# Rotary embedding on one core: the two tables loaded as sixteen rows each and spread by TensorE

## The chip, the cores and the metric

The kernel runs on one core of one Trainium2 chip. The time is what the device needs for one execution, in microseconds (us), as the median of several runs. A profiled execution of the same program gives what each engine and each transfer did; its times are read from the start of the span, that is, from the first to the last instruction.

Five engines work side by side, each through its own list of instructions: TensorE (PE), VectorE (DVE), ScalarE (ACT), GpSimd (POOL) and SyncE (SP). Transfers between memory and SBUF run on sixteen DMA engines, fed here by two queues: one that SyncE issues to (q1, "hardware_dynamic") and one that GpSimd issues to (q0, "software_dynamic"). A transfer that changes the type on its way, such as float32 in memory to float16 in SBUF, is issued by GpSimd here.

## The reference

The rotary embedding of x (8 batches, 2048 positions, 16 heads, 64 elements a head, float32) with tables cos and sin of 2048 x 32 float32:

```
x1 = x[..., :32]
x2 = x[..., 32:]
out1 = x1 * cos - x2 * sin      # cos, sin by position, the same for each batch and head
out2 = x1 * sin + x2 * cos
out = concatenate([out1, out2], axis=-1)
```

x is 67.1 MB and so is the output; a table is 256 KB.

## The kernel before, in words

Each batch is a tile of 128 partitions. Partition p holds the positions 16p to 16p + 15 (J = 16), so 16 x 1024 elements; in memory that is 64 KB in one piece for each partition. The load (`load`, line 54, GpSimd) casts to float16 on the way in, the store (`store`, line 62, GpSimd) casts back to float32 on the way out. The tiles come from a ring of five buffers, `io_pool`, tag "xt".

`rotate` (lines 67 to 83) is three VectorE passes over a tile: line 75 multiplies the swapped halves by the sine with its sign (`sin_h`, 128 x 16 x 64 float16) into `v`, line 81 multiplies the tile by the cosine (`cos_h`, 128 x 512 float16) in place, line 83 adds `v`.

At the start SyncE issues three transfers, in this order: the sine table (line 42, `sin_f`), the first four positions of each partition of batch 0 as float32 (line 43, `head`, 2 MB), and the cosine table (line 47, `cos_f`). A table is loaded as 128 rows of 2 KB, one for each partition: partition p gets its own 16 positions x 32 values. GpSimd at once issues the load of the rest of batch 0 and that of batch 1 (line 54).

ScalarE then makes the float16 tables and casts the head: the sine (line 94), the sine with its sign turned (line 95), position 0 of the head (`narrow_head`, line 89), the cosine (line 97), positions 1 to 3 of the head (line 89 again). VectorE rotates position 0 of batch 0 by itself (`rotate(tiles[0], 0, JF)`, line 99), and GpSimd stores it (line 108) before it issues loads 2, 3 and 4. That order of GpSimd's transfers (load 0, load 1, the first store, loads 2 to 4) is fixed by dependencies that hold no wait ("order of the ring", lines 115 to 121).

After that, batch by batch, VectorE rotates and GpSimd stores; the load of batch b + 5 takes over the buffer of batch b when its store has landed. The last batch goes out in three parts: two by GpSimd (lines 136 and 138), and the last two positions cast to float32 by ScalarE (line 147) and stored by SyncE (line 148), behind the first part.

Of the kernel before, what the change touches and what calls it, by code (L numbers as in the profile page):

```python
# [1 line left out]

# [4 lines left out]


@with_exitstack  # L10
def kernel(
    ctx: ExitStack,
    tc: tile.TileContext,
    x: bass.AP,
    cos: bass.AP,
    sin: bass.AP,
    out: bass.AP,
):
    nc = tc.nc
    f16 = mybir.dt.float16  # L20
    f32 = mybir.dt.float32

    B, S, H, D = x.shape
    Dh = D // 2
    P = nc.NUM_PARTITIONS
    J = S // P
    NBUF = 5

    const_pool = ctx.enter_context(tc.tile_pool(name="rope_const", bufs=1))
    io_pool = ctx.enter_context(tc.tile_pool(name="rope_io", bufs=NBUF))  # L30
    tmp_pool = ctx.enter_context(tc.tile_pool(name="rope_tmp", bufs=1))

    JA = 4
    JE = 2
    JF = 1
    head = io_pool.tile([P, JA, H, D], f32, tag="xt")
    x0 = x[0].rearrange("(p j) h d -> p j (h d)", j=J)
    sin_f = const_pool.tile([P, J, Dh], f32)
    cos_f = const_pool.tile([P, J, Dh], f32)
    cos_h = const_pool.tile([P, J, Dh], f16)  # L40
    sin_h = const_pool.tile([P, J, D], f16)
    nc.sync.dma_start(out=sin_f, in_=sin.rearrange("(p j) d -> p j d", j=J))  # L42
    nc.sync.dma_start(  # L43
        out=head.rearrange("p j h d -> p (j h d)"),
        in_=x0[:, 0:JA, :].rearrange("p j f -> p (j f)"),
    )
    nc.sync.dma_start(out=cos_f, in_=cos.rearrange("(p j) d -> p j d", j=J))

    loads = []

    def load(b):
        xt = io_pool.tile([P, J, H, D], f16, tag="xt")
        j0 = JA if b == 0 else 0
        dma = nc.gpsimd.dma_start(  # L54
            out=xt[:, j0:J, :, :].rearrange("p j h d -> p (j h d)"),
            in_=x[b].rearrange("(p j) h d -> p j (h d)", j=J)[:, j0:J, :].rearrange("p j f -> p (j f)"),
        )
        loads.append(dma)
        return xt

    def store(b, xt, j0=0):
        return nc.gpsimd.dma_start(  # L62
            out=out[b].rearrange("(p j) h d -> p j (h d)", j=J)[:, j0:J, :].rearrange("p j f -> p (j f)"),
            in_=xt[:, j0:J, :, :].rearrange("p j h d -> p (j h d)"),
        )

    def rotate(xt, j0, j1):
        v = tmp_pool.tile([P, J, H, D], f16)
        n = j1 - j0
        js = slice(j0, j1)  # L70
        shape = [P, n, H, 2, Dh]
        sin_b = sin_h[:, js, :].rearrange("p j (e d) -> p j e d", e=2).unsqueeze(2).to_broadcast(shape)
        cos_b = cos_h[:, js, :].unsqueeze(2).to_broadcast([P, n, 2 * H, Dh])
        xe = xt[:, js, :, :].rearrange("p j h (e d) -> p j h e d", e=2)
        nc.vector.tensor_mul(  # L75
            out=v[:, js, :, :].rearrange("p j h (e d) -> p j h e d", e=2),
            in0=xe[:, :, :, ::-1, :],
            in1=sin_b,
        )
        xw = xt[:, js, :, :].rearrange("p j h (e d) -> p j (h e) d", d=Dh)  # L80
        nc.vector.tensor_mul(out=xw, in0=xw, in1=cos_b)  # L81
        xa = xt[:, js, :, :].rearrange("p j h d -> p (j h d)")
        nc.vector.tensor_add(out=xa, in0=xa, in1=v[:, js, :, :].rearrange("p j h d -> p (j h d)"))  # L83


    tiles = [load(0)]
    tiles.append(load(1))
    def narrow_head(j0, j1):
        nc.scalar.copy(  # L89
            out=tiles[0][:, j0:j1, :, :].rearrange("p j h d -> p (j h d)"),  # L90
            in_=head[:, j0:j1, :, :].rearrange("p j h d -> p (j h d)"),
        )

    nc.scalar.copy(out=sin_h[:, :, Dh:D], in_=sin_f)  # L94
    nc.scalar.mul(out=sin_h[:, :, 0:Dh], in_=sin_f, mul=-1.0)  # L95
    narrow_head(0, JF)
    nc.scalar.copy(out=cos_h, in_=cos_f)  # L97
    narrow_head(JF, JA)
    rotate(tiles[0], 0, JF)
    def part(b, j0, j1):  # L100
        return (
            out[b].rearrange("(p j) h d -> p j (h d)", j=J)[:, j0:j1, :].rearrange("p j f -> p (j f)"),
            tiles[b][:, j0:j1, :, :].rearrange("p j h d -> p (j h d)"),
        )

    def store_rows(b, j0, j1):
        dst, src = part(b, j0, j1)
        return nc.gpsimd.dma_start(out=dst, in_=src)  # L108

    first = store_rows(0, 0, JF)  # L110
    ring = [loads[0], loads[1], first]
    for b in range(2, NBUF):
        tiles.append(load(b))
        ring.append(loads[b])
    for a, b in zip(ring[1:], ring[:-1]):
        tc.add_manual_dep(
            a.ins,
            b.ins.name,
            mybir.DependencyInfo(mybir.DependencyClass.NoSync, mybir.DependencyReason.DATA),
            reason="order of the ring",  # L120
        )
    for b in range(B):
        rotate(tiles[b], JF if b == 0 else 0, J)
        if b < B - 1:
            st = store(b, tiles[b], JF if b == 0 else 0)
            if b == 0:
                tc.add_manual_dep(
                    st.ins,
                    first.ins.name,
                    mybir.DependencyInfo(mybir.DependencyClass.NoSync, mybir.DependencyReason.DATA),  # L130
                    reason="order of the ring",
                )
        if b + NBUF < B:
            tiles.append(load(b + NBUF))
    dst, src = part(B - 1, 0, 9)
    gate = nc.gpsimd.dma_start(out=dst, in_=src)  # L136
    dst, src = part(B - 1, 9, J - JE)
    rest = nc.gpsimd.dma_start(out=dst, in_=src)  # L138
    tc.add_manual_dep(
        rest.ins,  # L140
        gate.ins.name,
        mybir.DependencyInfo(mybir.DependencyClass.NoSync, mybir.DependencyReason.DATA),
        reason="order of the ring",
    )
    dst, src = part(B - 1, J - JE, J)
    tail = io_pool.tile([P, JE, H, D], f32, tag="xt")
    nc.scalar.copy(out=tail.rearrange("p j h d -> p (j h d)"), in_=src)  # L147
    end = nc.sync.dma_start(out=dst, in_=tail.rearrange("p j h d -> p (j h d)"))
    tc.add_manual_dep(
        end.ins,  # L150
        gate.ins.name,
        mybir.DependencyInfo(mybir.DependencyClass.Sync, mybir.DependencyReason.DATA),
        reason="the last rows go out behind this part",
    )


# [1 line left out]
_INS = ['x', 'cos', 'sin']  # L158
_OUTS = [((8, 2048, 16, 64), 'float32')]


# [23 lines left out]
```

## Time and profile before

| What | Value |
|---|---|
| Time, median of 3 runs | 316.73 us (316.65 to 316.8) |
| Span of the profiled execution | 314.8 us |
| Time of the profiled execution beside its span | not given on the page; the median of the runs is 1.9 us above the span |
| VectorE busy | 209.1 us (66%), 27 instructions |
| ScalarE busy | 8.6 us (3%), 7 instructions |
| GpSimd busy | 9.9 us (3%), 22 instructions |
| TensorE | no instructions |
| Bytes in memory | 67.63 MB read, 67.11 MB written |
| Sine table: issue to landing | 2.8 us |
| Head: issue to landing | 16.4 us |
| Cosine table: issue to landing | 34.1 us |
| Load 0 (6 MB in memory): issue to landing | 22.0 us |
| First store (512 KB): issue to landing | 6.4 us |
| A VectorE pass over a whole tile, 128 x 16384 | 8.69 us |

The page gives each engine's busy time, the span in 40 slices (a digit is the busy share in tenths), the DMA queues with packets, megabytes and the time their packets took as a share of sixteen engines' span, and the chain of work that ended last. Answers of the trace add a timeline (start, duration, engine and line, what is written from what, and in brackets how long the engine had been idle and what ended that), and sums by stretch (busy time of each engine with the number of instructions in brackets, the clock that TensorE was granted, the DMA engines' share and the GB/s moved). In these GB/s, and in the queues' megabytes, a load that casts to float16 counts with the bytes it writes into SBUF, half of what it reads. Shares of a short stretch can exceed 1, because packets of two queues overlap on an engine.

### The profile page before, as it was taken

The numbers are of one execution on the slowest core, as the hardware profiler recorded it, in microseconds if no ns is written. First come the engines' busy times: TensorE is split into PE (matmuls) and PEld (weight loads), VectorE is DVE, ScalarE is ACT, GpSimd is POOL, SyncE is SP. The second block draws the span as 40 slices with busy tenths as digits, with TensorE's granted clock in tenths as the row PEclk, the third lists the DMA queues.
The fourth block names the chain that finished last, engine by engine and source line by source line (L and its number), as shares of the span: only waits on it lengthen the run. The fifth ranks groups of instructions, "written<-read, shape, count | busy, mean of one in ns | idle before, by whom it ended". The sixth has DMA issues, their size and how long they took to land.

```text
span 314.8 us, 126 instructions
## 1 busy us (share of the span) xinstructions
DVE 209.1 (66%) x27; ACT 8.6 (3%) x7; POOL 9.9 (3%) x22
## 2 busy tenths in 40 slices
DVE  0000299999999999999999999999009993000000
ACT  3010400000000000000000000000000002000000
POOL 1000110000000000010000000200000001000000
DMA  8999999999999899999999999999999999999998
GB/s 262 287 233 212 204 267 200 200 266 200 200 200 325 375 500 400 400 333 266 200 200 208 391 400 400 458 475 266 200 266 466 400 400 516 416 400 400 433 425 341
DMA packets 3168, 102.24 MB, mean 325 GB/s; under 512 B 352, under 2 KB 352, under 8 KB 736
## 3 DMA queue, kind: packets, MB, share of 16 engines
q0 software_dynamic: 2592, 98.57, 97.4%
q1 hardware_dynamic: 576, 3.67, 3.0%
HBM read 67.63 MB, written 67.11 MB: 428 GB/s over the span
## 4 chain that ended last, share of the span: by engine, by line
DMA 39%; DVE 24%; issue 18%; ACT 2%; POOL 0%; SPq 0%; POOLq 0%; DVEq 0%
DMA out_dram<-xt 16%; DMA xt<-in_x_dram 12%; DMA cos_f<-in_cos_dram 11%; DVE xt L83 8%; DVE xt L81 8%; DVE v L75 8%; ACT xt L89 1%; ACT tail L147 1%; POOL out_dram L62 0%; ACT cos_h L97 0%; POOL xt L54 0%; SPq L43 0%; SPq L42 0%; POOLq L54 0%; DVEq L75 0%
## 5 line engine op out<-in xcount | busy, mean ns | idle before, releaser
L75 DVE TENSOR_TENSOR v<-xt,sin_h 128x16384 f16<-128x16384 f16 (+2 forms) x9 | 69.7, 7744 | 35.9 <-ACT xt L89 19.8
L81 DVE TENSOR_TENSOR xt<-xt,cos_h 128x16384 f16<-128x16384 f16 (+2 forms) x9 | 69.7, 7744 | 17.4 <-ACT cos_h L97 17.1
L83 DVE TENSOR_TENSOR xt<-xt,v 128x16384 f16<-128x16384 f16 (+2 forms) x9 | 69.7, 7744 | 0.3
L147 ACT CAST tail<-xt 128x2048 f32<-128x2048 f16 x1 | 1.9, 1898 | 223.7 <-DVE xt L83 223.7
L54 POOL DMA_DIRECT2D xt<-in_x_dram x8 | 4.4, 555 | 105.4 <-DMA out_dram<-xt 104.6
L62 POOL DMA_DIRECT2D out_dram<-xt x7 | 3.7, 535 | 71.4 <-DVE xt L83 71.4
L89 ACT CAST xt<-head 128x1024 f16<-128x1024 f32 (+1 forms) x2 | 3.8, 1896 | 12.9 <-DMA head<-in_x_dram 12.9
L136 POOL DMA_DIRECT2D out_dram<-xt x1 | 0.5, 531 | 41.5 <-DVE xt L83 41.5
L108 POOL DMA_DIRECT2D out_dram<-xt x1 | 0.5, 536 | 35.7 <-DVE xt L83 35.7
L94 ACT ACT_TABLE_LOAD x1 | 1.3, 1283 | 0.7 <-PEq L169 0.7
L97 ACT CAST cos_h<-cos_f 128x512 f16<-128x512 f32 x1 | 0.6, 617 | 17.2 <-DMA cos_f<-in_cos_dram 17.2
L94 ACT CAST sin_h<-sin_f 128x512 f16<-128x512 f32 x1 | 0.6, 617 | 1.5 <-DMA sin_f<-in_sin_dram 1.5
L95 ACT ACTIVATE sin_h<-sin_f 128x512 f16<-128x512 f32 x1 | 0.6, 624 | 0.0
L138 POOL DMA_DIRECT2D out_dram<-xt x1 | 0.5, 531 | 0.0
L169 POOL MEMSET const-float32-0.0<- 128x1 f32 x1 | 0.1, 98 | 0.2 <-issue 0.2
L169 POOL MEMSET const-bfloat16-1.0<- 128x1 bf16 x1 | 0.1, 102 | 0.0
L169 POOL MEMSET const-float32-1.0<- 128x1 f32 x1 | 0.1, 98 | 0.0
L169 POOL MEMSET const-uint8-127<- 128x1 uint8 x1 | 0.1, 98 | 0.0
## 6 DMA issues: line engine op xcount, KB each, us to landing
xt<-in_x_dram POOLq DMA_DIRECT2D x7, 4096.0 KB, 38.3
out_dram<-xt POOLq DMA_DIRECT2D x1, 7680.0 KB, 56.7
out_dram<-xt POOLq DMA_DIRECT2D x1, 4608.0 KB, 42.4
xt<-in_x_dram POOLq DMA_DIRECT2D x1, 3072.0 KB, 22.0
out_dram<-xt POOLq DMA_DIRECT2D x1, 2560.0 KB, 47.9
head<-in_x_dram SPq DMA_DIRECT2D x1, 2048.0 KB, 16.4
out_dram<-tail SPq DMA_DIRECT2D x1, 1024.0 KB, 8.4
out_dram<-xt POOLq DMA_DIRECT2D x1, 512.0 KB, 6.4
```

Source lines behind the costliest of these rows:

```text
L54: dma = nc.gpsimd.dma_start(out=xt[:, j0:J, :, :].rearrange("p j h d -> p (j h d)"), in_=x[b].rearrange("(p j) h d -> p j (h d)", j=J)[:, ...
L62: return nc.gpsimd.dma_start(out=out[b].rearrange("(p j) h d -> p j (h d)", j=J)[:, j0:J, :].rearrange("p j f -> p (j f)"), in_=xt[:, j0:J ...
L75: nc.vector.tensor_mul(out=v[:, js, :, :].rearrange("p j h (e d) -> p j h e d", e=2), in0=xe[:, :, :, ::-1, :], in1=sin_b,)
L81: nc.vector.tensor_mul(out=xw, in0=xw, in1=cos_b)
L83: nc.vector.tensor_add(out=xa, in0=xa, in1=v[:, js, :, :].rearrange("p j h d -> p (j h d)"))
L89: nc.scalar.copy(out=tiles[0][:, j0:j1, :, :].rearrange("p j h d -> p (j h d)"), in_=head[:, j0:j1, :, :].rearrange("p j h d -> p (j h d)"),)
L94: nc.scalar.copy(out=sin_h[:, :, Dh:D], in_=sin_f)
L95: nc.scalar.mul(out=sin_h[:, :, 0:Dh], in_=sin_f, mul=-1.0)
L97: nc.scalar.copy(out=cos_h, in_=cos_f)
L108: return nc.gpsimd.dma_start(out=dst, in_=src)
L136: gate = nc.gpsimd.dma_start(out=dst, in_=src)
L147: nc.scalar.copy(out=tail.rearrange("p j h d -> p (j h d)"), in_=src)
```

## The change

Each table is loaded as sixteen rows of 16 KB instead of 128 rows of 2 KB. Row k holds the positions of partitions 8k to 8k + 7, and lands on partition k of a new tile `wide`, 16 x 2 x 8 x 512 float32, which takes a buffer of the ring (`io_pool`, tag "xt"). VectorE casts a table's part of `wide` to float16 in `narrow`, which shares its buffer with `v`. TensorE then makes the tile of 128 partitions: for each g of 8 one matmul with 512 columns, whose weights `pick[:, g, :]` are 1 where the output partition is 8k + g and 0 elsewhere, all eight summed into one PSUM tile. ScalarE's casts read PSUM instead of `sin_f` and `cos_f`.

`pick` is made from `ones` (set by VectorE) by one select on GpSimd. In the built program GpSimd has two instructions ahead of its first load that it had not before: a reload of its code library and the select. On VectorE the memset of `ones` and the two table casts stand ahead of the first rotation. On ScalarE the second cast of the head now stands ahead of the cast of the cosine; it was behind it. SyncE's order is as before: sine, head, cosine, and at the end the last rows. GpSimd's order of loads and stores is as before.

```
+    K = 16
+    G = P // K
     head = io_pool.tile([P, JA, H, D], f32, tag="xt")
+    wide = io_pool.tile([K, 2, G, J * Dh], f32, tag="xt")
+    narrow = tmp_pool.tile([K, 2, G, J * Dh], f16, tag="v")
-    sin_f = const_pool.tile([P, J, Dh], f32)
-    cos_f = const_pool.tile([P, J, Dh], f32)
+    ones = const_pool.tile([K, G, P], f16)
+    pick = const_pool.tile([K, G, P], f16)
+    psum_pool = ctx.enter_context(tc.tile_pool(name="rope_psum", bufs=1, space=bass.MemoryType.PSUM))
-    nc.sync.dma_start(out=sin_f, in_=sin.rearrange("(p j) d -> p j d", j=J))
+    nc.sync.dma_start(
+        out=wide[:, 0, :, :].rearrange("k g f -> k (g f)"), in_=sin.rearrange("(k r) d -> k (r d)", k=K)
+    )
     nc.sync.dma_start(
         out=head.rearrange("p j h d -> p (j h d)"),
...
-    nc.sync.dma_start(out=cos_f, in_=cos.rearrange("(p j) d -> p j d", j=J))
+    nc.sync.dma_start(
+        out=wide[:, 1, :, :].rearrange("k g f -> k (g f)"), in_=cos.rearrange("(k r) d -> k (r d)", k=K)
+    )
...
-        v = tmp_pool.tile([P, J, H, D], f16)
+        v = tmp_pool.tile([P, J, H, D], f16, tag="v")
...
-    nc.scalar.copy(out=sin_h[:, :, Dh:D], in_=sin_f)
-    nc.scalar.mul(out=sin_h[:, :, 0:Dh], in_=sin_f, mul=-1.0)
+    nc.vector.memset(ones, 1.0)
+    nc.gpsimd.affine_select(
+        out=pick,
+        in_=ones,
+        pattern=[[-1, G], [1, P]],
+        compare_op=mybir.AluOpType.is_equal,
+        fill=0.0,
+        base=0,
+        channel_multiplier=-G,
+    )
+
+    def spread(t):
+        nc.vector.tensor_copy(
+            out=narrow[:, t, :, :].rearrange("k g f -> k (g f)"), in_=wide[:, t, :, :].rearrange("k g f -> k (g f)")
+        )
+        ps = psum_pool.tile([P, J * Dh], f32, tag=f"ps{t}")
+        for g in range(G):
+            nc.tensor.matmul(ps, lhsT=pick[:, g, :], rhs=narrow[:, t, g, :], start=g == 0, stop=g == G - 1)
+        return ps.rearrange("p (j d) -> p j d", j=J)
+
+    sin_p = spread(0)
+    nc.scalar.copy(out=sin_h[:, :, Dh:D], in_=sin_p)
+    nc.scalar.mul(out=sin_h[:, :, 0:Dh], in_=sin_p, mul=-1.0)
     narrow_head(0, JF)
-    nc.scalar.copy(out=cos_h, in_=cos_f)
+    cos_p = spread(1)
+    nc.scalar.copy(out=cos_h, in_=cos_p)
     narrow_head(JF, JA)
```

## The prediction

> **What bounds the kernel now.** I read the page first, then the transfers in two short windows, then the engines and transfers stage by stage, and last the order of the start. The page's transfer lines come first:
>
> ```profile
> DMA  8999999999999899999999999999999999999998
> ...
> q0 software_dynamic: 2592, 98.57, 97.4%
> q1 hardware_dynamic: 576, 3.67, 3.0%
> HBM read 67.63 MB, written 67.11 MB: 428 GB/s over the span
> ```
>
> The sixteen DMA engines are busy in every slice, and the two queues' packets together take the whole span; VectorE has 66%. So the time is bytes over a rate, plus whatever time the DMA engines stand idle. By stages (stretch, length, busy time of DVE, ACT and POOL, clock, DMA share, GB/s on the SBUF side, where a cast load counts half):
>
> ```profile
> 1.75:5.25 3.50, 0.00 (x0) 1.42 (x3) 0.70 (x2) 1.00 1.00 375
> 17.50:42.50 25.00, 5.47 (x4) 4.32 (x3) 2.12 (x4) 1.00 0.97 210
> 42.50:140.00 97.50, 97.12 (x12) 0.00 (x0) 1.61 (x3) 1.00 1.03 307
> 140.00:305.00 165.00, 106.50 (x13) 1.90 (x1) 4.76 (x9) 1.00 1.00 357
> 305.00:313.50 8.50, 0.00 (x0) 0.00 (x0) 0.00 (x0) 1.00 0.98 405
> ```
>
> No stage has a hole. The rate while the engines run is (67.63 + 67.11) MB over 313.5 - 1.8 = 311.7 us, 432 GB/s. The stretch that the change is about, 17.5 to 42.5, looks bad from the compute side and is not:
>
> ```profile
> 3.52 0.62 ACT L94 CAST sin_h<-sin_f 128x512 f16<-128x512 f32 x1 [1.49 <-DMA sin_f<-in_sin_dram]
> ...
> 17.54 1.04 ACT L89 CAST xt<-head 128x1024 f16<-128x1024 f32 x1 [12.87 <-DMA head<-in_x_dram]
> ...
> 35.80 0.62 ACT L97 CAST cos_h<-cos_f 128x512 f16<-128x512 f32 x1 [17.22 <-DMA cos_f<-in_cos_dram]
> ...
> 38.16 0.54 POOL L108 DMA_DIRECT2D out_dram<-xt  x1 [35.71 <-DVE xt L83]
> 38.69 1.59 POOL L54 DMA_DIRECT2D xt<-in_x_dram  x3
> ```
>
> The head lands at 17.5 and the cosine at 35.8, so the first store and the three loads behind it are issued only at 38.16. But GpSimd's queue still holds the second load then: all that is ahead (0.26 + 2.10 + 6.29 + 0.26 + 8.39 = 17.3 MB) takes 40 us at 432 GB/s, to 41.8, and the share over 17.5 to 42.5 is 0.97. The cosine is late by a lot, and nothing in the transfers waits for it.
>
> The start is where something can be lost. Queues with packets in 0 to 5.25, then issues:
>
> ```profile
> q1 hardware_dynamic: 208, 1.31, 66.6%
> ```
>
> ```profile
> 0.74 0.37 SPq L42 DMA_DIRECT2D sin_f<-in_sin_dram  x1
> 1.16 0.42 SPq L43 DMA_DIRECT2D head<-in_x_dram  x1
> 1.25 1.20 POOL L54 DMA_DIRECT2D xt<-in_x_dram  x2 [0.81 <-PEq L180]
> 1.63 0.42 SPq L47 DMA_DIRECT2D cos_f<-in_cos_dram  x1
> ```
>
> Until 5.25 only SyncE's queue (q1) moves data; GpSimd's first load, issued at 1.25, sends no packet for 4.0 us. SyncE's first packets leave 1.0 us after their issue. The head start of SyncE's queue is the cover that the change draws on.
>
> **The parts of the change, with costs.**
> *GpSimd.* Ahead of its first load it now has a reload of its code library and the select that builds `pick`, which waits for VectorE's memset of `ones`. Queued behind both are load 0 and load 1, on which 97.4% of the transfers hang. No row shows a reload. Below it is nothing (the library may be there already); above, I take 8.4 us, the longest landing on queue q1 of a transfer of 1 MB (the tail's). I take 5.8: if it is a fetch that GpSimd causes, it has GpSimd's 4.0 us from issue to first packet and the 1.8 us that the sine took from first packet to landing (1.75 to 3.52). [...] The select on 16x1024 has no row either: between 0.69 (a VectorE pass of 1024 elements) and 2.75 (ScalarE's cast of 3072); GpSimd has no row near, so the middle, 1.7. The memset, under 0.7 us from 0.75, lies beside the reload; without a reload it costs GpSimd 0.2.
> So load 0 is issued at 0.75 + 5.8 + 1.7 = 8.25 instead of 1.25, and with the same 4.0 us its first packet leaves at 12.25 (at 9.3 if the lag were SyncE's 1.0).
>
> *What covers it.* SyncE's queue alone: 0.26 + 2.10 + 0.26 = 2.62 MB from 1.8 on, 6.1 us at 432 GB/s (to 7.9) or 7.0 us at the start's 375 (to 8.8); I take 8.3. So the DMA engines stand idle from 8.3 to 12.25, 3.95 us, and as they are never idle later, the end moves by the same.
>
> *The tables' transfers.* 256 KB each as before, 16 descriptors for 128. The fewer packets can save at most the difference of the two rates, 0.70 - 0.61 = 0.1 us each. That the rows land on 16 partitions only may cost: between nothing and a rate in proportion to the partitions, 8 x 0.61 = 4.9 us each. I take nothing, since SyncE's queue could run 3.95 us longer before the end moved by it, and keep the other end as a rival.
>
> *Cosine earlier.* With one row per DMA engine the cosine lands right behind the head, about 8.5 instead of 35.8. Its new work: a VectorE copy of 16x4096 (2.2 us from 8.69 us for 16384; 1.1 to 4.3), eight matmuls of 512 columns (no PE row; 4096 columns at VectorE's and ScalarE's paces for as many give 2.2 to 3.8, take 3.8), ScalarE's 0.62. Sine: landed 3.5, copied 5.7, `pick` ready 8.25, spread 12.1, two ScalarE casts 13.3. ScalarE then does both head casts (1.04 + 2.75) to 17.1, then the cosine, whose matmuls end at 15.9, to 17.7. On VectorE the first short pass (L75) is now queued behind the cosine's copy, which costs it nothing, as that copy ends near 11 and the pass needs ScalarE's head cast (14.3). The two other short passes give a first store near 19.2 instead of 38.16. That is worth nothing: load 0 and load 1 (14.7 MB, 34 us) fill the queue to 46. If this chain came more than 27 us later than I think, it would matter.
>
> *Buffers.* `wide` takes a buffer of the ring of five, so the fourth load waits for the head's casts and the fifth for the two table copies, both done by 18 us, before that ring position is issued. From the second store on the order of GpSimd's queue is as before, VectorE is ahead of its old times (tile 0 done near 51, not 63.7), and its later wait is for the last load.
>
> *Sum.* +3.95 for the idle stretch, the rest hidden or about 0: the profiled span of 314.8 becomes 318.8. The page gives that execution no time beside its span; the median of the runs is 316.73, 1.9 above it, and I keep that difference: 320.7 us.
>
> **The rivals.**
> 1. *Not slower: the cover is enough.* If GpSimd's first load is late by less than 8.3 - 5.25 = 3.05 us, the queue from SyncE is still running when it starts and no idle arises. Without a real reload the load is issued at 0.95 + 0.5 + 1.7 = 3.15, 1.9 us late: 316.7, or 316.5 with the packets' saving. For it: reloading what is loaded can be free. Against: a reload instruction stands in the built program, and the kernel before has none. The same case can end faster by a little: if taking turns between two queues is why the share is 0.97 in 17.5 to 42.5 and 1.00 later, 3% of 25 us come back, 316.0.
> 2. *VectorE holds GpSimd.* The cosine's copy would run at about 8.5 to 10.7, as GpSimd writes the descriptors of load 0. If those wait, 2.2 us more: 322.9. In this profile GpSimd issues many DMAs beside VectorE's passes with two inputs and each takes the usual 0.53 us, which speaks against; a one-input copy is not among them. [...]
> 3. *Narrow landing.* If the rows drain in proportion to 16 of 128 partitions, each table takes 4.3 us more and holds back what is queued on its engines: up to 8.6 us, 325.3. [...] The trace cannot show it: all its transfers span 128 partitions.
> 4. *A longer reload*, 8.4, and a select of 2.75: 2.6 + 1.05 more, 324.4.
>
> **How the numbers follow.** Forecast 0.48 (318.5 to 322); VectorE's lock 0.12; narrow landing 0.13; longer reload 0.07; cover enough 0.20, of which 0.14 within 0.2% (0.63 us, about what this measurement tells from no change) and 0.06 below. So slower 0.80. The predicted time is the forecast's, 320.7. The range leaves out the cover's case and the last bit of the narrow landing: 317.2 to 325.0.
>
> **What the profile after should show.** GpSimd's select starting near 6.6 us and its first load near 8.3; a stretch of DMA share 0 between about 8.5 and 12; the head landing near 8 instead of 17.5, the cosine right behind it; the first store before 25 us; every later stage at the shares above, and the last load landing some 4 us later. The prediction is wrong if the first load is issued before 4 us, if the transfers show no empty stretch, or if shares below 0.95 appear where both tables land.

## The result and the profile after

The changed kernel takes 319.45 us (319.36 to 319.68) against 316.75 us for the kernel before in the same measurement: a ratio of 1.0087, 95% interval 1.0074 to 1.01, 2.7 us slower. The span of the profiled execution grew from 314.8 to 317.7 us.

The page of the changed kernel, its transfer lines:

```profile
DMA  9999999999999999999999999999999999999997
...
q0 software_dynamic: 2592, 98.57, 96.7%
q1 hardware_dynamic: 352, 3.67, 3.5%
HBM read 67.63 MB, written 67.11 MB: 424 GB/s over the span
```

The bytes are the same and every slice is full; 96.7% and 3.5% still make up the whole span. There is no empty stretch. SyncE's queue (q1) has 352 packets where it had 576, and yet they took a larger share, 3.5% of a longer span: 11.1 us of sixteen engines instead of 9.4.

The changed kernel by the same stages (stretch, length, busy time of PE, its weight loads, DVE, ACT and POOL, clock, DMA share, GB/s on the SBUF side):

```profile
1.75:5.25 3.50, 0.00 (x0) 0.10 (x1) 0.34 (x2) 0.34 (x1) 2.27 (x3) 1.00 1.01 225
17.50:42.50 25.00, 3.57 (x8) 0.95 (x7) 15.32 (x6) 3.98 (x3) 2.13 (x4) 1.00 0.97 204
42.50:140.00 97.50, 0.00 (x0) 0.00 (x0) 97.12 (x12) 0.00 (x0) 1.61 (x3) 1.00 1.03 306
140.00:305.00 165.00, 0.00 (x0) 0.00 (x0) 98.93 (x12) 1.90 (x1) 4.75 (x9) 1.00 1.01 356
305.00:313.50 8.50, 0.00 (x0) 0.00 (x0) 0.00 (x0) 0.00 (x0) 0.00 (x0) 1.00 0.97 399
```

The first row is the finding: between 1.75 and 5.25 the DMA engines are as busy as before (1.01 against 1.00) and move 225 GB/s instead of 375. From 42.5 on the share and the rate of each row are within 2% of the old ones. So the loss is at the start, in engines that are busy and slow, not idle.

The start of the changed kernel, in its timeline:

```profile
0.81 0.37 SPq L47 DMA_DIRECT2D wide<-in_sin_dram  x1
1.07 0.91 DVE L103 MEMSET ones<- 16x1024 f16 x1 [1.07 <-PEq L200]
...
2.06 1.08 POOL L104 TENSOR_SCALAR_AFFINE_SELECT pick<-ones 16x1024 f16<-16x1024 f16 x1 [1.55 <-DVE ones L103]
3.10 1.23 POOL L63 DMA_DIRECT2D xt<-in_x_dram  x2
...
5.14 2.28 DVE L115 CAST narrow<-wide 16x4096 f16<-16x4096 f32 x1 [3.16 <-DMA wide<-in_sin_dram]
...
17.20 3.70 ACT L98 CAST xt<-head 128x1024 f16<-128x1024 f32 x2 [5.04 <-DMA head<-in_x_dram]
23.26 2.28 DVE L115 CAST narrow<-wide 16x4096 f16<-16x4096 f32 x1 [15.84 <-DMA wide<-in_cos_dram]
...
31.77 0.54 POOL L139 DMA_DIRECT2D out_dram<-xt  x1 [27.43 <-DVE xt L92]
```

The select starts 0.08 us after the memset that it waits for (1.07 + 0.91 = 1.98): a reload of the library takes no time that shows. Whatever it takes fits into the 1.55 us for which GpSimd waited for the memset. GpSimd's first load is issued at 3.10, 1.85 us later than before, not 7. The sine lands 4.3 us after its issue (2.8 before), the cosine at 23.2 (35.8 before), and the first store is issued 6.4 us earlier, at 31.77. That the cosine comes 12.6 us sooner has no effect on the end, as the transfers were full all the time.

### The profile page after: what moved, and what is told of

Its sections match the earlier page's. It is cut to its first block, busy times and chain, and to the rows that moved or that the text cites. A ratio compares the mean times of both kernels' runs of the same rounds, so it can differ in the third digit from the quotient of the medians.

```text
span 317.7 us, 168 instructions
## 1 busy us (share of the span) xinstructions
PE 7.1 (2%) x16; PEld 2.2 (1%) x16; DVE 214.6 (68%) x30; ACT 8.5 (3%) x7; POOL 11.0 (3%) x23
## 3 DMA queue, kind: packets, MB, share of 16 engines
q0 software_dynamic: 2592, 98.57, 96.7%
## 4 chain that ended last, share of the span: by engine, by line
DVE 26%; DMA 19%; another core or an unknown queue 18%; issue 18%; PE 1%; POOL 1%; ACT 1%; SPq 0%; DVEq 0%; POOLq 0%; ACTq 0%
DMA xt<-in_x_dram 12%; DVE xt L90 8%; DVE xt L92 8%; DVE v L84 8%; DMA wide<-in_cos_dram 7%; PE ps L120 1%; DVE narrow L115 1%; ACT tail L178 1%; POOL out_dram L71 0%; POOL xt L63 0%; SPq L50 0%; SPq L47 0%; DVEq L84 0%; POOLq L63 0%
## 5 line engine op out<-in xcount | busy, mean ns | idle before, releaser
L115 DVE CAST narrow<-wide 16x4096 f16<-16x4096 f32 x2 | 4.6, 2280 | 19.0 <-DMA wide<-in_cos_dram 15.8
L120 PE MATMUL ps<-narrow,pick 16*128 16x512 f16 x16 | 7.1, 622 | 22.0 <-DVE narrow L115 22.0
L120 PEld LDWEIGHTS <-pick 16*128 16x128 f16 x16 | 2.2, 136 | 26.1 <-issue 22.9
L103 DVE MEMSET ones<- 16x1024 f16 x1 | 0.9, 912 | 1.1 <-PEq L200 1.1
L104 POOL TENSOR_SCALAR_AFFINE_SELECT pick<-ones 16x1024 f16<-16x1024 f16 x1 | 1.1, 1082 | 1.6 <-DVE ones L103 1.6
```

What stands on the lines that cost most here:

```text
L103: nc.vector.memset(ones, 1.0)
L104: nc.gpsimd.affine_select(out=pick, in_=ones, pattern=[[-1, G], [1, P]], compare_op=mybir.AluOpType.is_equal, fill=0.0, base=0, channel_mu ...
L115: nc.vector.tensor_copy(out=narrow[:, t, :, :].rearrange("k g f -> k (g f)"), in_=wide[:, t, :, :].rearrange("k g f -> k (g f)"))
L120: nc.tensor.matmul(ps, lhsT=pick[:, g, :], rhs=narrow[:, t, g, :], start=g == 0, stop=g == G - 1)
```

## The experiments

Two theories. A: sixteen rows of 16 KB on the partitions 0 to 15 land slowly and hold up the DMA engines, which carry everything else too. B: GpSimd's later first load is what costs. The first four kernels ran together on one chip. The kernel before scattered there (316.39 to 320.38 in 34 of its 35 runs), so the four are compared with each other, and the one with the select alone, 316.6 us, serves as zero; in the other measurements the median of the kernel before was 316.56 to 316.75.

**Loads first.** The changed kernel, GpSimd's select behind its first two loads:

```
-    nc.gpsimd.affine_select(
+    sel = nc.gpsimd.affine_select(
...
+    tc.add_manual_dep(sel.ins, loads[1].ins.name, ...)   # no wait, order only
```

> The changed kernel with GpSimd's library reload and select moved behind its first two loads, so that load 0 is again issued near 1.25 us; the tables still land as sixteen rows on 16 partitions. Theory A (the sixteen rows land slowly and hold the DMA engines): the loss stays, 319.4 us, within 0.4. Theory B (GpSimd's first load is issued 1.85 us later, and the DMA engines do less until it comes): the loss goes, 316.7 us. If both carry a part, between 317.3 and 318.8.

318.96 us (318.41 to 319.66). GpSimd issues load 0 at 1.31 again, and the loss stays. B does not explain it.

**The select alone.** The kernel before, with the memset and the select ahead of GpSimd's first load:

```
+    nc.vector.memset(ones, 1.0)
+    sel = nc.gpsimd.affine_select(out=pick, in_=ones, ...)
     tiles = [load(0)]
...
+    tc.add_manual_dep(loads[0].ins, sel.ins.name, ...)   # no wait, order only
```

> The kernel before with only the memset and the select added, ahead of GpSimd's first load, which is then issued near 3.1 us instead of 1.25; nothing reads what the select makes, and the tables land as 128 rows as before. Theory A (slow landing of sixteen rows): no change, 316.7 us, within 0.3, since SyncE's own queue covers the first 8 us. Theory B (late first load): the whole loss appears, 319.4 us.

316.60 us (316.48 to 317.05), the kernel before's own time. Here too load 0 is issued at 3.10; it costs nothing. These two runs settle B.

**Only the sine as sixteen rows.** The changed kernel with the cosine's line and cast as before:

```
+    cos_f = const_pool.tile([P, J, Dh], f32)
...
-    nc.sync.dma_start(out=wide[:, 1, :, :]..., in_=cos.rearrange("(k r) d -> k (r d)", k=K))
+    nc.sync.dma_start(out=cos_f, in_=cos.rearrange("(p j) d -> p j d", j=J))
...
-    cos_p = spread(1)
+    cos_p = cos_f
```

> The changed kernel with the cosine loaded as before (128 rows of 2 KB, no spreading); only the sine comes as sixteen rows; GpSimd's select stays ahead of its loads. Theory A: half of the loss, 318.1 us (1.3 to 1.4 for one table), or less if the start, where only SyncE's queue runs, hides it. Theory B: all of the loss, 319.4 us.

317.23 us (317.20 to 317.60): 0.6 us above the zero, a quarter of the loss, where A had expected half or less.

**Only the cosine as sixteen rows.** The same edit on the sine's lines.

> The changed kernel with the sine loaded as before; only the cosine comes as sixteen rows, in the middle of load 0; GpSimd's select stays ahead of its loads. Theory A: half of the loss, 318.1 us, and the packets of load 0 beside the cosine are slowed. Theory B: all of the loss, 319.4 us.

317.78 us (317.11 to 318.33): 1.2 us. Each table costs by itself, as A says, in a kernel that has only half of the casts and matmuls. The two make 1.8 us, while both together stand 2.4 us above the zero in the run with the loads first; why the pair costs 0.6 more than its parts stays open.

The first 26 us show the slower transfers. The stretch 1.75 to 26, first of the kernel before (no TensorE columns), then of the changed kernel, of the cosine alone, and of the select alone (no TensorE columns):

```profile
1.75:26.00 24.25, 0.69 (x1) 2.47 (x4) 0.70 (x2) 1.00 1.07 277
```

```profile
1.75:26.00 24.25, 3.98 (x10) 1.35 (x11) 4.80 (x3) 5.12 (x5) 2.27 (x3) 1.00 1.07 253
```

```profile
1.75:26.00 24.25, 3.57 (x8) 1.05 (x8) 4.81 (x6) 5.77 (x6) 2.27 (x3) 1.00 1.03 261
```

```profile
1.75:26.00 24.25, 0.93 (x2) 2.52 (x4) 2.27 (x3) 1.00 1.07 280
```

The share is 1.07 in the kernels before and after alike, the rate 277 against 253. The missing 24 GB/s over 24.25 us are 0.58 MB on the SBUF side, and as the lagging bytes belong to cast loads, which count half, about 1.2 MB in memory: 2.7 us at the 432 GB/s of the prediction. That this is just the loss is chance. Around 26 GpSimd's packets start in groups of sixteen, 0.52 MB on the SBUF side (in the kernel before between 25.0 and 26.0, then none before 27.0), and one group more or less before 26 is 22 GB/s, or 2.4 us by the same working. The cosine alone, at 261, would lose 2.1 us by it against 280, not 1.2.

The size can be read without such an edge from the first store. In every kernel GpSimd's queue has load 0 and load 1 ahead of it, and SyncE's three transfers of the start have landed before it does; so it lands later by what was lost until then. Its time from issue to landing, before and after:

```profile
out_dram<-xt POOLq DMA_DIRECT2D x1, 512.0 KB, 6.4
```

```profile
out_dram<-xt POOLq DMA_DIRECT2D x1, 512.0 KB, 15.7
```

| Kernel (its profiled execution) | First store issued | Landed | Span |
|---|---|---|---|
| Before | 38.16 | 44.6 | 314.8 |
| Select alone | 33.71 | 45.1 | 315.3 |
| Changed | 31.77 | 47.5 | 317.7 |
| Loads first | 32.59 | 46.5 | 316.7 |
| Sine alone | 37.16 | 45.7 | 315.9 |
| Cosine alone | 26.05 | 45.4 | 315.6 |

In each row landing and span lie above the first row by the same, to 0.1 us. So the whole loss has arisen by the landing of the first store, and nothing is lost or won after it. These are single executions: that of the sine alone was the longest of its twelve runs and that of the cosine alone among the shortest, so what each table costs is taken from the medians.

**Four spare loads, three ways.** To price the landing without casts, matmuls or the select, the kernel before gets four more 256 KB loads on SyncE's queue behind the cosine, into the unused half of the head's buffer; nothing reads them:

```
+    for _ in range(4):
+        nc.sync.dma_start(out=spare[:, 0:512], in_=sin.rearrange("(p j) d -> p (j d)", j=J))      # 128 rows
+        nc.sync.dma_start(out=spare[0:16, :], in_=sin.rearrange("(k r) d -> k (r d)", k=16))      # 16 rows, partitions 0 to 15
+        nc.sync.dma_start(out=spare[::8, :], in_=sin.rearrange("(k r) d -> k (r d)", k=16))       # 16 rows, every eighth partition
```

(one of the three lines in each kernel; head and spare are the two halves of one tile, `room`)

> The kernel before with four more loads of a 256 KB table on SyncE's queue behind the cosine, one after the other, into the unused half of the head's buffer; nothing reads them. Here each comes as 128 rows of 2 KB on 128 partitions: the plain price of the bytes. 4 x 0.61 = 2.4 us more than the kernel before, 319.0 us, by every theory.

> As the run with four spare loads of 128 rows, but each as sixteen rows of 16 KB on the partitions 0 to 15. Theory A (rows on few partitions drain slowly and hold the engines): on top of the bytes' 2.4 us the excess of the cosine run (1.2 us above the kernel before, whose byte price is already in it), four times: 4.8 us, so 323.8 us, 2 us either way. If the loss in the changed kernel came from the casts, the matmuls or GpSimd's select, which are all absent here: 319.0 us, as with 128 rows.

> As the run with four spare loads of sixteen rows of 16 KB, but the rows land on every eighth partition (0, 8, ... 120) instead of 0 to 15: same rows, same sizes, same number. If it is the place of the rows that costs (neighbouring partitions share a way in), the excess over 128 rows shrinks to half or less: below 321.5 us. If it is that only sixteen long rows are sent, whatever their place: as with partitions 0 to 15, near 323.8 us.

Beside 316.56 us for the kernel before, the three took 326.13 (326.07 to 326.21), 324.64 (324.20 to 326.36) and 319.77 us (319.42 to 319.82).

The run with 128 rows is spoilt as a price. Its four loads went one after the other, each issued when the one before had landed, and took 43.4, 22.4, 17.6 and 2.5 us from issue to landing. GpSimd's fifth load of x, which takes over that buffer, waited until 88.7 with the first big store queued behind it, and GpSimd's queue ran empty. Its stretch 80 to 95 (busy time of DVE, ACT, POOL, clock, DMA share, GB/s), and the same stretch with sixteen rows:

```profile
80.00:95.00 15.00, 14.93 (x3) 0.00 (x0) 1.60 (x3) 1.00 0.64 135
```

```profile
80.00:95.00 15.00, 14.93 (x3) 0.00 (x0) 0.54 (x1) 1.00 0.99 214
```

0.36 of 15 us is 5.4 us of idle engines there, and nearly none with sixteen rows, whose loads had landed by 74. So the other two can be compared with each other: same rows, same sizes, same number, only the partitions differ, and the neighbouring ones cost 4.9 us more, 1.2 us a load, the price of the cosine alone. It is the place of the rows, not that only sixteen long rows are sent. Against the bytes' price of 2.4 us, which is worked out from 432 GB/s and not measured, rows on every eighth partition are dear by 0.8 us in all, 0.2 a load, and neighbouring ones by 5.7, 1.4 a load. Why neighbouring partitions are dearer no run shows; what the runs show is that the place of the rows decides, 324.64 us on the partitions 0 to 15 and 319.77 us on every eighth.

**More rows.** The changed kernel with K = 32 and K = 64, and the changed kernel again on their chip, beside 316.63 us for the kernel before:

```
-    K = 16
+    K = 32        # or 64
```

> The changed kernel with each table as 32 rows of 8 KB on the partitions 0 to 31, and four matmuls instead of eight; the copy on VectorE is half as long. Theory A with a price by the place of the rows: the excess falls to half or a third of the changed kernel's 2.7 us: 317.4 to 318.0. If the loss does not hang on the number of partitions: 319.4.

> The changed kernel with each table as 64 rows of 4 KB on the partitions 0 to 63, two matmuls. If the price goes with the number of partitions: a quarter of 2.7, 317.3 or less, below the run with 32 rows. [...]

> The changed kernel itself on the chip of the runs with 32 and 64 rows, so that they can be compared directly: 319.4 us.

316.64 us for 32 rows (eleven of twelve runs 316.48 to 317.03, one 319.32), 316.94 for 64, 318.91 (318.34 to 319.78) for the changed kernel; the ratios to the kernel before are 1.0 (0.9979 to 1.0021), 1.0008 (0.9994 to 1.0023) and 1.0068 (1.0044 to 1.0093). The loss is gone with 32 partitions, with order, select, casts and matmuls still in place (the last three about half as long as with sixteen: 0.62 us for 1.08, 1.21 for 2.28, 1.86 for 3.57), and 64 gain nothing over 32. That is sharper than a halving: A's expectation for 32 rows (317.4 to 318.0) was too high. With 32 rows each row is shorter too, 8 KB, but the run with every eighth partition has 16 KB rows and loses little, so the length is not the cause. What 32 partitions may still lose is less than the measurement can tell: 0.01 us between the medians. The first store lands at 44.8 and 45.0, 0.2 and 0.4 us later than in the kernel before, as their spans of 315.0 and 315.2 are longer. The stretch 1.75 to 26 with 32 rows, then with 64:

```profile
1.75:26.00 24.25, 3.72 (x8) 1.03 (x8) 3.13 (x4) 5.70 (x6) 1.59 (x3) 1.00 1.09 281
```

```profile
1.75:26.00 24.25, 1.01 (x2) 0.31 (x3) 0.69 (x1) 5.12 (x5) 1.10 (x2) 1.00 1.00 261
```

With 32 rows it is 281 GB/s, the rate of the kernel before. With 64 it is 261, as with the cosine alone, and next to nothing is lost: the edge at 26 again. The first store with 32 rows goes out at 27.70, 10.5 us earlier than before the change, and the time is the same: an early cosine is worth nothing here. Neither version beat the kernel before.

**Six selects.** What the forecast had thought to be the cause, made real: the kernel before with six selects ahead of the first load.

```
+    for _ in range(6):
+        sel = nc.gpsimd.affine_select(out=pick, in_=ones, ...)
     tiles = [load(0)]
...
+    tc.add_manual_dep(loads[0].ins, sel.ins.name, ...)   # no wait, order only
```

> The kernel before with the select six times ahead of GpSimd's first load instead of once, so that load 0 is issued near 8.7 us and sends its first packet near 12.8; tables as 128 rows. This tests the cover that the forecast used: if the DMA engines stand idle from the end of SyncE's own queue (8.3) until GpSimd's first packet, 4.5 us are lost: 321.1 us. If a late first load costs nothing at all: 316.6 us.

319.18 us (319.12 to 319.24), 2.6 more than the kernel before, not 4.5. Load 0 is issued at 8.85. The queues until 10.25, then the stretch just before and the quarter of a microsecond behind it (busy time of DVE, ACT, POOL, clock, DMA share, GB/s):

```profile
q1 hardware_dynamic: 432, 2.62, 65.5%
q0 software_dynamic: 1, 0.02, 1.4%
```

```profile
8.75:10.25 1.50, 0.69 (x1) 1.50 (x3) 1.33 (x3) 1.00 0.10 16
```

```profile
10.25:10.50 0.25, 0.23 (x1) 0.25 (x1) 0.00 (x0) 1.00 7.03 1081
```

By 10.25 SyncE's 2.62 MB are through and GpSimd's first packet has just left: 1.4 us after the issue, not 4.0. So the 4.0 us of the kernel before were not all GpSimd's own: some 2.6 of them go with the packets of SyncE's queue that were under way on the same engines. How an engine shares its time between the queues is not shown. The idle stretch is about 1.4 us (0.90 of 1.5). The other 1.2 us of the 2.6 are not accounted for; they too are lost by the landing of the first store (47.3, 2.7 us later than before).

The last row also tells how to read the shares: SyncE's queue is through, and the share is 7.03 with GpSimd's queue alone. So a packet counts with its whole time in the stretch in which it starts, and a share above 1 in a short stretch need not come from two queues.

## Why the prediction was right or wrong

*The sign and the range held, the mechanism did not.* 319.45 lies in 317.2 to 325.0, and in the forecast's own 318.5 to 322, but by the third rival's way, to which 0.13 was given. That the number came close is luck: 3.95 us of idle engines that never came stood in the sum where 2.7 us of slow landing should have stood. Two of the three signs by which the prediction was to be known as wrong came: the first load was issued before 4 us (3.10), and the transfers show no empty stretch.

*What bounds the kernel*: right. The transfers are full in both profiles, and the time goes with what the DMA engines lose.

*GpSimd's reload, 5.8 us*: the step that failed. It took nothing that shows: the select began 0.08 us after the memset, at 2.06, and GpSimd had idled for 1.55 us in all. I had set the price by analogy between a low end of nothing and a high end of 8.4 us; nothing was the answer. The select, 1.7 in the sum, was 1.08.

*GpSimd's lag of 4.0 us to its first packet*: carried over to a place where it does not hold. It is 1.4 us with SyncE's queue empty, as the sum had it empty from 8.3 on. The trace of before could not show that, as both queues started together, but the sum should have kept the lag as an open bound on that account and not as a constant.

*The cover until 8.3*: right in size. With six selects SyncE's queue is done by 8.75, and a load 1.85 us late costs nothing (316.60). Rival 1 was right on this point: issue at 3.15 forecast, 3.10 measured.

*The landing, taken as nothing*: the other failed step, and the whole loss: 0.6 us for the sine, 1.2 for the cosine, 2.3 to 2.7 together. I took zero because the idle stretch would hide it; with no idle stretch nothing did. Rival 3 gave 325.3 by an upper bound in proportion to the partitions, 8.6 us for the two tables; they cost 2.3 to 2.7.

*VectorE's copy holding GpSimd*: not tested. GpSimd's first load was issued at 3.10, before the sine's copy (5.14 to 7.42), and nothing from GpSimd fell on the cosine's. GpSimd's first packets left between 7.25 and 7.5, 4.2 to 4.4 us after the issue; in the kernel before, which has no such copy, it was 4.0 us.

*Cosine earlier, worth nothing*: right, though the times were off. The cosine landed at 23.2, not 8.5, as load 0's packets came between (with six selects, where they come later, it landed at 9.0), and the first store went out at 31.77, not 19.2. The run with 32 rows shows the worth: 10.5 us earlier for no time at all. The casts (2.28 for 2.2) and the matmuls (3.57 for 3.8) were sized well.

## What to carry to other kernels

When the DMA engines are busy all the time, ask of each transfer not only how many bytes and packets it has, but over how many partitions, and which, it lands: the same 256 KB cost nothing extra that could be measured on 32 or 64 partitions (316.64 and 316.94 us beside 316.63), and 0.6 to 1.4 us on the first sixteen. Engines that are busy and slow looked here like engines that are busy, a share of 1.01 at 225 GB/s beside 1.00 at 375; read the rate beside the share, stretch by stretch, and take the size of a loss from a landing behind the same bytes, as a stretch's edge cuts through groups of packets. And work that reached its engine earlier was worth nothing here, where the queue that sets the end never ran dry without it: with 32 rows the first store went out 10.5 us earlier, for 316.64 us beside 316.63.

## What was not expected of the hardware

The library reload on GpSimd cost no visible time. GpSimd's first packet left 1.4 us after its issue with the other queue empty (issue at 8.85 with six selects), 4.0 us after it with packets of that queue under way in the kernel before, and 4.2 to 4.4 us after it in the changed kernel (issued at 3.10, no packet by 7.25). The same sixteen rows cost 0.2 us a load above their bytes on every eighth partition and 1.4 us on the partitions 0 to 15 (8.1 - 2.4 = 5.7 us for four), but 32 neighbouring partitions were already as good as 128 (316.64 us beside 316.63).
